# A squared-ReLU MLP in split float32: the second product turned round, 512 weight columns moving, and its halves alternated with the first product

## Chip, cores and metric

The kernel runs on one core of a Trainium2 chip. The metric is device time in microseconds, the median over runs of the whole program; the profile is one execution taken by the hardware profiler. Engines are named as the profile names them: PE (TensorE matmul), PEld (its weight loads), DVE (VectorE), ACT (ScalarE), POOL (GpSimd), SP (SyncE, which issues the loads).

## What is computed

One residual layer over 512 tokens of width 2048, in float32. Attention, a gated unit and their merge come first and are untouched. The end of the layer is the part that matters here:

```python
x = x + merged @ w_out[l]
h2 = rms_norm(x, g_ff[l])
x = x + jnp.square(jax.nn.relu(h2 @ w_ff1[l])) @ w_ff2[l]   # w_ff1 2048 x 8192, w_ff2 8192 x 2048
```

## The kernel before

Every float32 operand is split into a high and a low piece (`split_to`: ACT casts the high piece, DVE subtracts it from the source to get the low one), and each product is three matmuls, high*high, high*low and low*high (`mm3`, lines 64 to 66). So each line of `mm3` appears in the trace once for each product tile.

The program is written as straight Python loops; a tile framework places semaphores, gives out buffers and fixes the order on each engine ahead of the run. Buffers of 128 x 512 float32 come from one pool, `slots` (81 of them). Weights arrive in `w_raw` (three buffers), and their split pieces and sums live in `w_piece` (six buffers of 4 KB a partition). PSUM has eight banks, five `acc` and three `aux`.

The MLP walks the 8192 hidden columns in eight chunks of 1024, each of four pairs of 128-column blocks. `hidden(f, p)` makes one pair: `by_column` holds pieces of `w_ff1` (128 x 128) stationary and moves the 512 tokens of `h2T`; 96 matmuls; DVE applies the ReLU and the row scale out of PSUM (line 584), ACT squares. `factors` forms four further combinations of the pair's quarters on POOL (lines 596 to 599) and splits seven operands into `ys`.

`strassen` then does the second product as a two-by-two block product with seven block products instead of eight. It runs once for each chunk and each 256 output columns (eight passes a chunk, 64 in all). A pass loads eight 128-row blocks of `w_ff2` in two transfers, POOL adds the four weight sums (line 156), ACT and DVE split each of the seven weight operands (lines 99 and 100), and PE runs 7 x 4 x 3 = 84 matmuls: weight piece stationary, 256 tokens of `ys` moving, so the result is transposed (output column on the partition). After each block product DVE adds the PSUM result into `x2T`, the residual held transposed (line 624), one or two additions of 128 x 256. In the last chunk PE turns every finished block back (line 633), ACT copies it out of PSUM, and SP stores it. `x2T` is made earlier by `turned`: four transposes for each of 16 column blocks, which `h2T` needs too, and one ACT copy (line 562).

The first hidden pair of the next chunk is computed ahead of the passes of this one (`early`), so a chunk on PE is four `hidden` in a row and then eight passes in a row.

Of the kernel before, what the change touches and what calls it, by code (L numbers as in the profile page):

```python
# [9 lines left out]
F32 = mybir.dt.float32  # L10
F32R = mybir.dt.float32r
AF = mybir.ActivationFunctionType
ALU = mybir.AluOpType
AX = mybir.AxisListType

P = 128
D = 2048
S = 512
NTB = S // P
KT = D // P  # L20
# [5 lines left out]
EPS = 1e-6  # L26
CK = 2
W = 512


@with_exitstack
def tile_hybrid_layer(ctx: ExitStack, tc: tile.TileContext, x, g_mix, w_in, g_q, g_k, ln_g, ln_b,
# [4 lines left out]
    nc = tc.nc  # L37

    const = ctx.enter_context(tc.tile_pool(name="const", bufs=1))
    wpool = ctx.enter_context(tc.tile_pool(name="wpool", bufs=3))  # L40
    small = ctx.enter_context(tc.tile_pool(name="small", bufs=8))
    slots = ctx.enter_context(tc.tile_pool(name="slots", bufs=81))
    ps_acc = ctx.enter_context(tc.tile_pool(name="ps_acc", bufs=5, space=bass.MemoryType.PSUM))
    ps_aux = ctx.enter_context(tc.tile_pool(name="ps_aux", bufs=3, space=bass.MemoryType.PSUM))

    def slot(name, dt=F32):
        return slots.tile([P, 512], dt, name=name, tag="slot")

    def acc(name):
        return ps_acc.tile([P, 512], F32, name=name, tag="acc")  # L50

    def aux(name):
        return ps_aux.tile([P, 512], F32, name=name, tag="aux")
# [8 lines left out]
    def mm3(o, lh, rh, start, stop, **kw):  # L62

        nc.tensor.matmul(o, lhsT=lh[0], rhs=rh[0], start=start, stop=False, **kw)  # L64
        nc.tensor.matmul(o, lhsT=lh[0], rhs=rh[1], start=False, stop=False, **kw)  # L65
        nc.tensor.matmul(o, lhsT=lh[1], rhs=rh[0], start=False, stop=stop, **kw)  # L66

    state = {"load": None}
# [19 lines left out]
        nc.vector.tensor_tensor(out=lo, in0=raw, in1=f32(hi), op=ALU.subtract)  # L88
        return hi, lo

    def split(src, name, scale=None):

        hi, lo = slot(name + "_hi", F32R), slot(name + "_lo", F32R)
        split_to(hi, lo, src, scale)
        return hi, lo

    def split_to(hi, lo, src, scale=None):
        if scale is None:
            nc.scalar.copy(out=hi, in_=src)  # L99
            nc.vector.tensor_tensor(out=lo, in0=src, in1=f32(hi), op=ALU.subtract)  # L100
        else:
            nc.scalar.activation(out=hi, in_=src, func=AF.Copy, scale=scale)
            nc.vector.scalar_tensor_tensor(out=lo, in0=src, scalar=scale, in1=f32(hi),
                                           op0=ALU.mult, op1=ALU.subtract)

    early = []
# [26 lines left out]
        for c in range(w // P):  # L133
            evac(c, o[c])

    def strassen(wap, r0, c0, rhs, evac):

        KH = 4
        half = []
        for h in range(2):
            raw = wpool.tile([P, KH, 2, P], F32, name="w_raw", tag="w_raw", bufs=3)
            state["load"] = nc.sync.dma_start(
                out=raw.rearrange("p k h c -> p k (h c)"),
                in_=wap[r0:r0 + 2 * KH * P, c0:c0 + 2 * P].rearrange("(k h p) c -> h p k c", p=P, h=2)[h])
            half.append(raw)  # L150
        w11, w21 = half[0][:, :, 0, :], half[0][:, :, 1, :]
        w12, w22 = half[1][:, :, 0, :], half[1][:, :, 1, :]
        sums = [wpool.tile([P, 2, KH, P], F32, name="w_sum", tag="w_piece", bufs=6) for _ in range(2)]
        sa, sc, sd, sb = sums[0][:, 0], sums[0][:, 1], sums[1][:, 0], sums[1][:, 1]
        for o, a, b in ((sa, w11, w21), (sc, sa, w22), (sd, sc, w12), (sb, w21, w22)):
            nc.gpsimd.tensor_tensor(out=o, in0=a, in1=b, op=ALU.add)  # L156
        banks = [acc("q") for _ in range(4)]
        for w, name, b, first, last in ((w11, "y11", 0, True, False), (w12, "y21", 1, True, True),
                                        (sa, "m7", 2, True, False), (sc, "m6", 0, False, False),
                                        (sd, "y22", 3, True, True), (w22, "m4", 2, False, True),  # L160
                                        (sb, "m5", 0, False, True)):
            both = wpool.tile([P, 2, KH, P], F32R, name="w_both", tag="w_piece", bufs=6)
            split_to(both[:, 0], both[:, 1], w)
            o = banks[b][:, :2 * P]
            for k in range(KH):
                mm3(o, (both[:, 0, k, :], both[:, 1, k, :]), rhs(k, name), first and k == 0, k == KH - 1,
                    skip_group_check=True)
            evac(name, o)


    warm = const.tile([P, 1], F32, name="warm")
# [2 lines left out]
    ident = const.tile([P, P], F32, name="ident")  # L174
# [76 lines left out]
    def hT_of(k):  # L251

        if k == len(hT):
            t = aux("xT")
            for tb in range(NTB):
                nc.tensor.transpose(out=t[:, tb * P:(tb + 1) * P], in_=xq[tb, k], identity=ident)
            hT.append(split(t, "hT", gT[:, k:k + 1]))
        return hT[k]

    def scale_of_x():  # L260
# [262 lines left out]
    for j in range(D // W):  # L523
        g = gb.pop(0) if gb else gate(GA + D + j * W, "gb")
        flush()

        def evac_b(c, o):
            m = slot("merged")
            nc.vector.tensor_tensor(out=m, in0=o, in1=g[c], op=ALU.mult)
            nc.gpsimd.tensor_tensor(out=m, in0=m, in1=merged_a[j * 4 + c], op=ALU.add)  # L530
            mT.append(split(m, "mT"))

        by_column(w_ob[0], j * W, lambda k: sT[k], SGW // P, evac_b, "yb")


    x2 = {}
    x2T = []
    h2T = []
    ss2 = const.tile([P, NTB, 4], F32, name="ss2")
    for j in range(D // W):  # L540
        def evac_x(tb, o):
            t = x2[tb, j]
            nc.vector.tensor_tensor(out=t, in0=o, in1=t, op=ALU.add)
            sq = slot("sq")
            nc.scalar.activation(out=sq, in_=t, func=AF.Square, accum_out=ss2[:, tb, j:j + 1])

        ref = state["load"]
        with tc.issue_after(ref.ins):
            for tb in range(NTB):
                t = slot("x2")  # L550
                nc.sync.dma_start(out=t, in_=x[tb * P:(tb + 1) * P, j * W:(j + 1) * W])
                x2[tb, j] = t
        by_token(w_out[0], j * W, lambda k: mT[k], KT, evac_x, "xo")

        def turned(c, j=j):
            t = aux("x2T")
            for tb in range(NTB):
                nc.tensor.transpose(out=t[:, tb * P:(tb + 1) * P], in_=x2[tb, j][:, c * P:(c + 1) * P],
                                    identity=ident)
            k = j * 4 + c  # L560
            keep = slot("x2T")
            nc.scalar.copy(out=keep, in_=t)
            x2T.append(keep)
            h2T.append(split(t, "h2T", gT2[:, k:k + 1]))

        behind.extend([lambda c=c, turned=turned: turned(c) for c in range(4)])
# [3 lines left out]
    rstd2 = rsqrt(ms2, 4, "rstd2")  # L570
    behind.append(lambda: along(rstd2, rstd_b))


    HS = S // 2
    PAIRS = 4
    chunks = DFF // (PAIRS * 2 * P)

    def hidden(f, p):
# [26 lines left out]
            split_to(*y[name], src)  # L605
        return y

    early = hidden(0, 0)
    for f in range(chunks):
        ys = [factors(early)]  # L610
        ys += [factors(hidden(f, p)) for p in range(1, PAIRS)]
        if f < chunks - 1:

            early = hidden(f + 1, 0)
        for j in range(D // (2 * P)):
            ca, cb = x2T[2 * j], x2T[2 * j + 1]
            a11, a12, a21, a22 = ca[:, :HS], ca[:, HS:], cb[:, :HS], cb[:, HS:]
            takes = {"y11": [(a11, ALU.add)], "y21": [(a11, ALU.add)], "m7": [(a22, ALU.add)],
                     "m6": [(a21, ALU.subtract)], "y22": [(a12, ALU.add)], "m4": [(a21, ALU.add)],
                     "m5": [(a22, ALU.subtract), (a12, ALU.add)]}  # L620

            def evac_y(name, o):
                for a, op in takes[name]:
                    nc.vector.tensor_tensor(out=a, in0=a, in1=o, op=op)  # L624

            strassen(w_ff2[0], f * PAIRS * 2 * P, j * 2 * P, lambda k, name: ys[k][name], evac_y)
            if f == chunks - 1:
                for pb in range(2):
                    t = aux("xo")
                    for b in range(2):  # L630
                        for c in range(2):
                            tb = pb * 2 + b
                            nc.tensor.transpose(out=t[:, (b * 2 + c) * P:(b * 2 + c + 1) * P],
                                                in_=(ca, cb)[c][:, tb * P:(tb + 1) * P], identity=ident)
                    r = slot("out")
                    nc.scalar.copy(out=r, in_=t)
                    nc.sync.dma_start(
                        out=out[pb * 2 * P:(pb + 1) * 2 * P, j * 2 * P:(j + 1) * 2 * P]
                        .rearrange("(b p) c -> p b c", p=P),
                        in_=r.rearrange("p (b c) -> p b c", b=2))  # L640


# [23 lines left out]
```

## Time and profile before

| what | us |
|---|---|
| median of three runs (2591.97 to 2593.3) | 2592.62 |
| the profiled execution | 2592.95 |
| its span, first to last instruction | 2591.2 |

The span is what the rows below are measured in; the profiled execution's own time is 1.75 us more than its span. Engine "busy" is the union of instruction times. Matmuls overlap in the records (a new one starts before the record of the last one ends), so the pace of PE is read from start to start and not from the mean duration.

### The profile page before, as it was taken

The numbers are of one execution on the slowest core, as the hardware profiler recorded it, in microseconds if no ns is written. First come the engines' busy times: TensorE is split into PE (matmuls) and PEld (weight loads), VectorE is DVE, ScalarE is ACT, GpSimd is POOL, SyncE is SP. The second block draws the span as 40 slices with busy tenths as digits, with TensorE's granted clock in tenths as the row PEclk, the third lists the DMA queues.
The fourth block names the chain that finished last, engine by engine and source line by source line (L and its number), as shares of the span: only waits on it lengthen the run. The fifth ranks groups of instructions, "written<-read, shape, count | busy, mean of one in ns | idle before, by whom it ended". The sixth has DMA issues, their size and how long they took to land.

```text
span 2591.2 us, 34954 instructions
## 1 busy us (share of the span) xinstructions
PE 2572.0 (99%) x14058; PEld 2235.7 (86%) x14058; DVE 1399.7 (54%) x2030; ACT 906.7 (35%) x1428; POOL 606.6 (23%) x507
## 2 busy tenths in 40 slices
PE   8999999999999999999999999999999999999999
PEld 7888888888888888888899898898998988989989
DVE  4555563333335333333567486584774856847666
ACT  5333342222223222233333343343333433433334
POOL 0211110000201100000143252351522624415233
PEclk9999999999999999999999999999999999999999
DMA  5332322333332333433333333233232332333333
GB/s 171 90 90 74 90 72 91 97 98 98 114 112 84 98 98 98 129 107 107 97 86 115 93 90 114 84 104 110 87 114 90 99 113 83 115 98 90 112 90 117
DMA packets 204419, 260.24 MB, mean 100 GB/s; under 512 B 8368, under 2 KB 146656, under 8 KB 204256
## 3 DMA queue, kind: packets, MB, share of 16 engines
q1 hardware_dynamic: 204256, 258.01, 33.3%
q8 instruction: 110, 1.80, 0.3%
q14 instruction: 53, 0.43, 0.1%
HBM read 253.78 MB, written 4.19 MB: 100 GB/s over the span
## 4 chain that ended last, share of the span: by engine, by line
PE 97%; DVE 2%; issue 0%; DMA 0%; ACT 0%; SPq 0%; POOL 0%; DVEq 0%; ACTq 0%; POOLq 0%
PE q L64 9%; PE q L66 9%; PE q L65 9%; PE f L65 9%; PE f L66 9%; PE f L64 9%; PE xo L66 2%; PE xo L64 2%; PE xo L65 2%; PE gb L64 2%; PE gb L65 2%; PE gb L66 2%; PE ga L64 2%; PE ga L66 2%; PE ga L65 2%; PE v L66 1%
## 5 line engine op out<-in xcount | busy, mean ns | idle before, releaser
L88 DVE TENSOR_TENSOR w_lo<-w_raw,w_hi 128x1024 fp32r<-128x1024 f32 x336 | 415.4, 1236 | 826.5 <-ACT w_hi L86 813.1
L86 ACT CAST w_hi<-w_raw 128x1024 fp32r<-128x1024 f32 x336 | 353.6, 1052 | 951.5 <-PE f L65 248.4
L64 PE MATMUL q<-ys,w_both 128*128 128x256 f32 x1792 | 505.4, 285 | 3.0 <-DVE x2T L624 0.6
L65 PE MATMUL q<-ys,w_both 128*128 128x256 f32 x1792 | 501.8, 283 | 0.1
L66 PE MATMUL q<-ys,w_both 128*128 128x256 f32 x1792 | 491.1, 284 | 3.5 <-DVE w_both L100 3.5
L64 PE MATMUL f<-h2T_hi,w_hi 128*128 128x512 f32 x1024 | 398.7, 389 | 0.0
L65 PE MATMUL f<-h2T_lo,w_hi 128*128 128x512 f32 x1024 | 398.4, 389 | 0.0
L66 PE MATMUL f<-h2T_hi,w_lo 128*128 128x512 f32 x1024 | 397.4, 389 | 0.0
L64 PEld LDWEIGHTS q<-ys,w_both 128*128 128x128 f32 x1792 | 342.9, 191 | 10.4 <-issue 8.9
L65 PEld LDWEIGHTS q<-ys,w_both 128*128 128x128 f32 x1792 | 343.3, 192 | 0.8 <-DVE ys L100 0.3
L66 PEld LDWEIGHTS q<-ys,w_both 128*128 128x128 f32 x1792 | 335.4, 192 | 6.8 <-DVE w_both L100 6.8
L156 POOL TENSOR_TENSOR w_sum<-w_raw 128x512 f32<-128x512 f32 x128 | 185.0, 1452 | 261.3 <-PE q L66 169.1
L624 DVE TENSOR_TENSOR x2T<-x2T,q 128x256 f32<-128x256 f32 x512 | 198.6, 410 | 78.5 <-PE q L66 77.4
L100 DVE TENSOR_TENSOR w_both<-w_raw,w_both 128x512 fp32r<-128x512 f32 x192 | 193.3, 1030 | 67.5 <-ACT w_both L99 67.5
L65 PEld LDWEIGHTS f<-h2T_lo,w_hi 128*128 128x128 f32 x1024 | 192.2, 188 | 39.7
L66 PEld LDWEIGHTS f<-h2T_hi,w_lo 128*128 128x128 f32 x1024 | 192.2, 188 | 39.6
L64 PEld LDWEIGHTS f<-h2T_hi,w_hi 128*128 128x128 f32 x1024 | 192.3, 188 | 39.4
L100 DVE TENSOR_TENSOR w_both<-w_sum,w_both 128x512 fp32r<-128x512 f32 x256 | 217.5, 869 | 1.3 <-ACT w_both L99 1.2
L99 ACT CAST w_both<-w_sum 128x512 fp32r<-128x512 f32 x256 | 157.8, 619 | 171.5 <-PE q L66 133.5
L99 ACT CAST w_both<-w_raw 128x512 fp32r<-128x512 f32 x192 | 118.1, 621 | 227.4 <-PE q L66 113.4
L156 POOL TENSOR_TENSOR w_sum<-w_sum,w_raw 128x512 f32<-128x512 f32 x128 | 183.1, 1431 | 5.0
L596 POOL TENSOR_TENSOR m<-relu 128x256 f32<-128x256 f32 x32 | 37.0, 1158 | 596.7 <-ACT relu L585 596.7
(202 smaller groups left out, 4088.3 us busy)
## 6 DMA issues: line engine op xcount, KB each, us to landing
w_raw<-in_w_ff_dram SPq DMA_DIRECT2D x256, 512.0 KB, 4.0
w_raw<-in_w_in_dram SPq DMA_DIRECT2D x144, 512.0 KB, 3.8
w_raw<-in_w_out_dram SPq DMA_DIRECT2D x32, 512.0 KB, 3.8
w_raw<-in_w_oa_dram SPq DMA_DIRECT2D x16, 512.0 KB, 3.8
w_raw<-in_w_ob_dram SPq DMA_DIRECT2D x16, 512.0 KB, 3.7
x<-in_x_dram SPq DMA_DIRECT2D x16, 256.0 KB, 5.0
out_dram<-out SPq DMA_DIRECT2D x16, 256.0 KB, 4.5
xq<-in_x_dram SPq DMA_DIRECT2D x12, 256.0 KB, 5.5
```

What stands on the lines that cost most here:

```text
L64: nc.tensor.matmul(o, lhsT=lh[0], rhs=rh[0], start=start, stop=False, **kw)
L65: nc.tensor.matmul(o, lhsT=lh[0], rhs=rh[1], start=False, stop=False, **kw)
L66: nc.tensor.matmul(o, lhsT=lh[1], rhs=rh[0], start=False, stop=stop, **kw)
L86: nc.scalar.copy(out=hi, in_=raw)
L88: nc.vector.tensor_tensor(out=lo, in0=raw, in1=f32(hi), op=ALU.subtract)
L99: nc.scalar.copy(out=hi, in_=src)
L100: nc.vector.tensor_tensor(out=lo, in0=src, in1=f32(hi), op=ALU.subtract)
L156: nc.gpsimd.tensor_tensor(out=o, in0=a, in1=b, op=ALU.add)
L596: nc.gpsimd.tensor_tensor(out=m7, in0=y12, in1=y22, op=ALU.subtract)
L624: nc.vector.tensor_tensor(out=a, in0=a, in1=o, op=op)
```

## The change

The second product now holds the activations stationary, 128 tokens at a time, and moves 512 columns of weights, so that a result lies token on the partition, as `x2` itself lies. A chunk is two pairs (512 hidden columns, 16 chunks); the block product is now over two halves of the tokens and two 512-column halves of a 1024-column output half, so there are two passes a chunk (`g` = 0, 1), 32 in all. A pass is 7 block products x 2 token tiles x 2 pairs x 3 = 84 matmuls of 512 columns. It loads four quarters of `w_ff2` (128 x 2 x 512 each) into a new pool `whole` of five buffers; the four weight sums are made on POOL one by one, three of them in place over a quarter, each before the operand that needs it. Each block product has two PSUM results of 128 x 512, each added by DVE into `x2` in one or two additions (16 in a pass). `x2T` with its copies, the final transposes and the copies out are gone; the stores go from `x2`. The order is `hidden` of the next chunk's first pair, pass 0 of this chunk, `hidden` of the second pair, pass 1. `slots` shrinks to 72; ten buffers of a pool `spare` hold the first pieces of `hT` and the last of `mT`, and their room is given to `whole` afterwards.

```diff
+SLOTS = 72
+SPARE = 10
...
-    def strassen(wap, r0, c0, rhs, evac):
-        KH = 4
-        half = []
-        for h in range(2):
-            raw = wpool.tile([P, KH, 2, P], F32, name="w_raw", tag="w_raw", bufs=3)
...
-        for o, a, b in ((sa, w11, w21), (sc, sa, w22), (sd, sc, w12), (sb, w21, w22)):
-            nc.gpsimd.tensor_tensor(out=o, in0=a, in1=b, op=ALU.add)
-        banks = [acc("q") for _ in range(4)]
...
-            both = wpool.tile([P, 2, KH, P], F32R, name="w_both", tag="w_piece", bufs=6)
-            split_to(both[:, 0], both[:, 1], w)
-            o = banks[b][:, :2 * P]
-            for k in range(KH):
-                mm3(o, (both[:, 0, k, :], both[:, 1, k, :]), rhs(k, name), first and k == 0, k == KH - 1,
-                    skip_group_check=True)
-            evac(name, o)
+    def strassen(wap, r0, c0, lhs, evac):
+        KH = 2
+        def piece(name):
+            return wpool.tile([P, KH, W], F32R, name=name, tag="w_piece", bufs=6)
+        def whole(name):
+            return state["whole"].tile([P, KH, W], F32, name=name, tag="whole")
+        def quarter(h, c):
+            raw = whole("w_raw")
             state["load"] = nc.sync.dma_start(
+                out=raw, in_=wap[r0:r0 + 2 * KH * P, c0 + c * W:c0 + (c + 1) * W]
+                .rearrange("(k h p) c -> h p k c", p=P, h=2)[h])
+            return raw
+        w11, w12, w21, w22 = quarter(0, 0), quarter(1, 0), quarter(0, 1), quarter(1, 1)
+        sc = whole("w_sum")
+        def plus(o, a, b):
             nc.gpsimd.tensor_tensor(out=o, in0=a, in1=b, op=ALU.add)
+        made = {"m7": lambda: plus(w11, w11, w21), "m6": lambda: plus(sc, w11, w22),
+                "y22": lambda: plus(w12, sc, w12), "m5": lambda: plus(w21, w21, w22)}
+        take = {"y11": w11, "y21": w12, "m7": w11, "m6": sc, "y22": w12, "m4": w22, "m5": w21}
+        banks = {}
+        for name, b, first, last in (("y11", 0, True, False), ("y21", 1, True, True),
+                                     ("m7", 2, True, False), ("m6", 0, False, False),
+                                     ("y22", 1, True, True), ("m4", 2, False, True),
+                                     ("m5", 0, False, True)):
+            if name in made:
+                made[name]()
+            hi, lo = piece("w_hi"), piece("w_lo")
+            split_to(hi, lo, take[name])
+            if first:
+                banks[b] = [(aux if b == 1 else acc)("q") for _ in range(2)]
+            for t in range(2):
+                o = banks[b][t]
+                for k in range(KH):
+                    y = [part[:, t * P:(t + 1) * P] for part in lhs(k, name)]
+                    mm3(o, y, (hi[:, k, :], lo[:, k, :]), first and k == 0, k == KH - 1,
+                        skip_group_check=True)
+                evac(name, t, o)
...
-            keep = slot("x2T")
-            nc.scalar.copy(out=keep, in_=t)
-            x2T.append(keep)
...
+    before.close()
+    state["whole"] = ctx.enter_context(tc.tile_pool(name="whole", bufs=5))
...
-    PAIRS = 4
+    PAIRS = 2
...
+    takes = {"y11": [(0, 0, ALU.add)], "y21": [(0, 0, ALU.add)], "m7": [(1, 1, ALU.add)],
+             "m6": [(0, 1, ALU.subtract)], "y22": [(1, 0, ALU.add)], "m4": [(0, 1, ALU.add)],
+             "m5": [(1, 1, ALU.subtract), (1, 0, ALU.add)]}
+    ahead = [hidden(0, p) for p in range(PAIRS)]
     for f in range(chunks):
...
+        ys = [factors(act) for act in ahead]
+        ahead = []
+        for g in range(2):
+            if f < chunks - 1:
+                ahead.append(hidden(f + 1, g))
+            def evac_y(name, t, o):
+                for half, c, op in takes[name]:
+                    a = x2[2 * half + t, 2 * g + c]
                     nc.vector.tensor_tensor(out=a, in0=a, in1=o, op=op)
...
-            if f == chunks - 1:
-                for pb in range(2):
-                    t = aux("xo")
...
+                    if f == chunks - 1 and (name, half, c) in (("m4", 0, 1), ("y21", 0, 0),
+                                                              ("m5", 1, 1), ("m5", 1, 0)):
+                        tb, j = 2 * half + t, 2 * g + c
+                        nc.sync.dma_start(out=out[tb * P:(tb + 1) * P, j * W:(j + 1) * W], in_=a)
+            strassen(w_ff2[0], f * PAIRS * 2 * P, g * 2 * W, lambda k, name: ys[k][name], evac_y)
```

## Rows read from the trace of the kernel before

**Rows 1.** The page's busy times by engine (share of the span, number of instructions) and its line of the granted TensorE clock in 40 slices, 9 being full speed.

```profile
PE 2572.0 (99%) x14058; PEld 2235.7 (86%) x14058; DVE 1399.7 (54%) x2030; ACT 906.7 (35%) x1428; POOL 606.6 (23%) x507
...
PEclk9999999999999999999999999999999999999999
```

**Rows 2.** The page's chain of work that ended last, shares of the span by engine; and what PE waited for in the whole span: total us, times, longest us.

```profile
PE 97%; DVE 2%; issue 0%; DMA 0%; ACT 0%; SPq 0%; POOL 0%; DVEq 0%; ACTq 0%; POOLq 0%
...
PE q L66 <- DVE w_both L100: 3.5, 9, 2.0
```

**Rows 3.** The matmuls of the first product (f) and of the second (q), by tile: number, duration ns min/median/max, first and last start, shape.

```profile
L64 PE MATMUL f<-h2T_hi,w_hi x1024: 389/389/473, 1215.2 to 2493.4; 128*128 128x512 f32 x171
...
L66 PE MATMUL f<-h2T_hi,w_lo x1024: 389/389/478, 1215.7 to 2493.8; 128*128 128x512 f32 x171
...
L66 PE MATMUL q<-ys,w_both x1792: 277/283/387, 1327.0 to 2585.5; 128*128 128x256 f32 x200
```

**Rows 4.** PE in order of time (start us, duration us): the first and the last of 92 successive matmuls of 512 columns, of which the earlier ones (xo) hold activations and move weights and the later ones (f) hold weights and move activations.

```profile
1199.82 0.39 PE L65 MATMUL xo<-w_lo,mT_hi 128*128 128x512 f32 x1
...
1220.44 0.40 PE L66 MATMUL f<-h2T_hi,w_lo 128*128 128x512 f32 x1
```

**Rows 5.** PE in order of time: the first and the last of 19 successive matmuls of 256 columns in a pass.

```profile
1504.74 0.28 PE L66 MATMUL q<-ys,w_both 128*128 128x256 f32 x1
...
1506.90 0.28 PE L64 MATMUL q<-ys,w_both 128*128 128x256 f32 x1
```

**Rows 6.** The chain of work that ended last, in order of time (start us, us): starts of passes of the first chunk (two of them four passes apart), then the last chunk with its final transposes, and the end.

```profile
1355.04 0.36 PE q L64
...
1396.50 0.35 PE q L64
...
2523.55 0.44 PE xo L633 x4
...
2578.25 0.44 PE xo L633 x4
2585.78 0.42 DVE x2T L624
...
2587.35 0.59 ACT out L636
```

**Rows 7.** Groups of instructions by line and shape: count, busy us, mean ns of one, idle time before them and what ended it.

```profile
L88 DVE TENSOR_TENSOR w_lo<-w_raw,w_hi 128x1024 fp32r<-128x1024 f32 x336 | 415.4, 1236 | 826.5 <-ACT w_hi L86 813.1
L86 ACT CAST w_hi<-w_raw 128x1024 fp32r<-128x1024 f32 x336 | 353.6, 1052 | 951.5 <-PE f L65 248.4
...
L156 POOL TENSOR_TENSOR w_sum<-w_raw 128x512 f32<-128x512 f32 x128 | 185.0, 1452 | 261.3 <-PE q L66 169.1
L624 DVE TENSOR_TENSOR x2T<-x2T,q 128x256 f32<-128x256 f32 x512 | 198.6, 410 | 78.5 <-PE q L66 77.4
L100 DVE TENSOR_TENSOR w_both<-w_raw,w_both 128x512 fp32r<-128x512 f32 x192 | 193.3, 1030 | 67.5 <-ACT w_both L99 67.5
...
L100 DVE TENSOR_TENSOR w_both<-w_sum,w_both 128x512 fp32r<-128x512 f32 x256 | 217.5, 869 | 1.3 <-ACT w_both L99 1.2
...
L156 POOL TENSOR_TENSOR w_sum<-w_sum,w_raw 128x512 f32<-128x512 f32 x128 | 183.1, 1431 | 5.0
...
L100 DVE TENSOR_TENSOR ys<-m,ys 128x256 fp32r<-128x256 f32 x128 | 71.1, 579 | 4.6 <-ACT ys L99 4.6
L100 DVE TENSOR_TENSOR ys<-relu,ys 128x256 fp32r<-128x256 f32 x96 | 70.0, 749 | 1.4 <-ACT ys L99 1.4
...
L584 DVE SCALAR_TENSOR_TENSOR relu<-f,rstd_b 128x512 f32<-128x512 f32 x64 | 44.3, 692 | 87.0 <-PE f L66 86.9
...
L543 DVE TENSOR_TENSOR x<-xo,x 128x512 f32<-128x512 f32 x16 | 11.0, 690 | 5.5 <-PE xo L66 4.0 <-DMA w_raw<-in_w_out_dram 0.7 <-DMA w_raw<-in_w_ff_dram 0.7
```

**Rows 8.** Three stretches: length, and for each engine its busy time and instructions, then granted clock, DMA share, GB/s. The first is four `hidden` with a pass at its end, the second passes alone, the third the last chunk's passes.

```profile
1413.00:1506.00 93.00, 93.00 (x449) 78.62 (x448) 43.44 (x58) 31.73 (x54) 24.01 (x23) 1.00 0.31 95
1506.00:1582.00 76.00, 75.48 (x607) 73.72 (x607) 68.78 (x115) 32.73 (x55) 37.61 (x26) 1.00 0.35 105
2494.00:2591.00 97.00, 89.59 (x738) 87.85 (x736) 67.48 (x126) 43.46 (x78) 40.08 (x32) 1.00 0.36 109
```

**Rows 9.** DVE and POOL in order of time within one pass: a split with no POOL instruction beside it, POOL's sums, and two splits that ran beside them.

```profile
1542.68 0.68 DVE L100 TENSOR_TENSOR w_both<-w_raw,w_both 128x512 fp32r<-128x512 f32 x1
...
1546.43 3.01 POOL L156 TENSOR_TENSOR w_sum<-w_sum,w_raw 128x512 f32<-128x512 f32 x2
...
1547.57 2.41 DVE L100 TENSOR_TENSOR w_both<-w_raw,w_both 128x512 fp32r<-128x512 f32 x2
```

**Rows 10.** DVE in order of time through one `hidden`: weight splits as pieces come free, and the ReLU of the same half of two successive `hidden`.

```profile
1421.49 1.23 DVE L88 TENSOR_TENSOR w_lo<-w_raw,w_hi 128x1024 fp32r<-128x1024 f32 x1 [4.21 <-ACT w_hi L86]
1426.93 1.23 DVE L88 TENSOR_TENSOR w_lo<-w_raw,w_hi 128x1024 fp32r<-128x1024 f32 x1 [4.21 <-ACT w_hi L86]
1428.79 0.69 DVE L584 SCALAR_TENSOR_TENSOR relu<-f,rstd_b 128x512 f32<-128x512 f32 x1 [0.64 <-PE f L66]
...
1450.55 0.69 DVE L584 SCALAR_TENSOR_TENSOR relu<-f,rstd_b 128x512 f32<-128x512 f32 x1 [0.63 <-PE f L66]
```

**Rows 11.** DMA issues: size and median us from issue to landing.

```profile
w_raw<-in_w_ff_dram SPq DMA_DIRECT2D x256, 512.0 KB, 4.0
...
out_dram<-out SPq DMA_DIRECT2D x16, 256.0 KB, 4.5
```

More of the change, by code (lines that the diff above doesn't have):

```diff
@@ L41, in tile_hybrid_layer, with slot @@
     small = ctx.enter_context(tc.tile_pool(name="small", bufs=8))
-    slots = ctx.enter_context(tc.tile_pool(name="slots", bufs=81))
+    slots = ctx.enter_context(tc.tile_pool(name="slots", bufs=SLOTS))
+    before = ExitStack()
+    spare = before.enter_context(tc.tile_pool(name="spare", bufs=SPARE))
     ps_acc = ctx.enter_context(tc.tile_pool(name="ps_acc", bufs=5, space=bass.MemoryType.PSUM))
     ps_aux = ctx.enter_context(tc.tile_pool(name="ps_aux", bufs=3, space=bass.MemoryType.PSUM))
-    def slot(name, dt=F32):
-        return slots.tile([P, 512], dt, name=name, tag="slot")
+    def slot(name, dt=F32, pool=slots):
+        return pool.tile([P, 512], dt, name=name, tag="slot")
     def acc(name):
@@ L89, in weight, with split @@
         return hi, lo
-    def split(src, name, scale=None):
-        hi, lo = slot(name + "_hi", F32R), slot(name + "_lo", F32R)
+    def split(src, name, scale=None, pool=slots):
+        hi, lo = slot(name + "_hi", F32R, pool), slot(name + "_lo", F32R, pool)
         split_to(hi, lo, src, scale)
@@ L134, in by_column @@
             evac(c, o[c])
-    def strassen(wap, r0, c0, rhs, evac):
-        KH = 4
-        half = []
-        for h in range(2):
-            raw = wpool.tile([P, KH, 2, P], F32, name="w_raw", tag="w_raw", bufs=3)
-            state["load"] = nc.sync.dma_start(
[L148 to L154, printed above, removed]
-        for o, a, b in ((sa, w11, w21), (sc, sa, w22), (sd, sc, w12), (sb, w21, w22)):
-            nc.gpsimd.tensor_tensor(out=o, in0=a, in1=b, op=ALU.add)
-        banks = [acc("q") for _ in range(4)]
[L158 to L161, printed above, removed]
-            both = wpool.tile([P, 2, KH, P], F32R, name="w_both", tag="w_piece", bufs=6)
-            split_to(both[:, 0], both[:, 1], w)
-            o = banks[b][:, :2 * P]
-            for k in range(KH):
-                mm3(o, (both[:, 0, k, :], both[:, 1, k, :]), rhs(k, name), first and k == 0, k == KH - 1,
-                    skip_group_check=True)
-            evac(name, o)
@@ L256, in hT_of @@
                 nc.tensor.transpose(out=t[:, tb * P:(tb + 1) * P], in_=xq[tb, k], identity=ident)
-            hT.append(split(t, "hT", gT[:, k:k + 1]))
+            hT.append(split(t, "hT", gT[:, k:k + 1], spare if k < SPARE // 2 else slots))
         return hT[k]
@@ L530, in evac_b @@
             nc.gpsimd.tensor_tensor(out=m, in0=m, in1=merged_a[j * 4 + c], op=ALU.add)
-            mT.append(split(m, "mT"))
+            mT.append(split(m, "mT", pool=spare if len(mT) >= KT - 4 else slots))
         by_column(w_ob[0], j * W, lambda k: sT[k], SGW // P, evac_b, "yb")
     x2 = {}
-    x2T = []
     h2T = []
@@ L606, in factors @@
         return y
-    early = hidden(0, 0)
+    takes = {"y11": [(0, 0, ALU.add)], "y21": [(0, 0, ALU.add)], "m7": [(1, 1, ALU.add)],
+             "m6": [(0, 1, ALU.subtract)], "y22": [(1, 0, ALU.add)], "m4": [(0, 1, ALU.add)],
+             "m5": [(1, 1, ALU.subtract), (1, 0, ALU.add)]}
+    ahead = [hidden(0, p) for p in range(PAIRS)]
     for f in range(chunks):
[L610 to L623, printed above, removed]
-                    nc.vector.tensor_tensor(out=a, in0=a, in1=o, op=op)
-            strassen(w_ff2[0], f * PAIRS * 2 * P, j * 2 * P, lambda k, name: ys[k][name], evac_y)
-            if f == chunks - 1:
-                for pb in range(2):
-                    t = aux("xo")
[L630 to L640, printed above, removed]
```

## Prediction, made before the changed kernel was run

> **What bounds the kernel now.** I read the shares of the engines first, then the chain that ended last and PE's waits, then the pace of PE from start to start, and last what the other engines do in the stretches of the second product. PE is busy 99% of the span at the full granted clock [rows 1], the chain is PE for 97%, and its largest wait in this product is 3.5 us in nine pieces, for DVE's weight splits [rows 2]. So time is gained only by giving PE less to do, and lost only where another engine makes PE wait.
>
> The pace is the point. 92 matmuls of 512 columns start within 20.62 us: 20.62 / 91 = 0.2266 us each, and this series runs over both orientations (weights moving, then activations moving) without a break [rows 4]. 19 matmuls of 256 columns take 2.16 us: 2.16 / 18 = 0.1200 us each [rows 5]. Two of these cost 0.2400 us, one wide one 0.2266 us: a matmul carries 13.4 ns that do not scale with its columns. A pass is 84 x 0.1200 = 10.08 us, but passes follow each other every (1396.50 - 1355.04) / 4 = 10.365 us [rows 6], so 0.285 us is lost at each pass. A `hidden` takes 1450.55 - 1428.79 = 21.76 us [rows 10], which is 96 x 0.2267.
>
> The other engines have slack on average and little inside the passes: DVE is busy 68.78 of 76 us there, and 43.44 of 93 us in the stretch of `hidden` [rows 8].
>
> **PE's share, worked out.** The multiplications are the same: 64 passes x 84 matmuls x 256 columns against 32 x 84 x 512. Before: 64 x 10.365 = 663.4 us. After: a pass is 84 x 0.2266 = 19.03 us, and I leave it the same loss at its start, 0.285 us, since it has as many instructions: 32 x 19.32 = 618.2 us. That is -45.2 us. The bounds are no loss per pass (-54.3) and 0.39 us more at each of some 31 changes from `hidden` to a pass, which is what the nine waits of 3.5 us make each [rows 2] (-45.2 + 12 = -33).
>
> The eight blocks of the last chunk are 10.94 us apart, (2578.25 - 2523.55) / 5, instead of 10.365 [rows 6]: the final transposes cost 8 x 0.575 = 4.6 us, and they go: -4.6 us. The 16 ACT copies into `x2T` and the ACT copies of the output go too; ACT is not on the chain [rows 2], so they are worth nothing. The 64 transposes into h2T stay, as does all of the first product.
>
> The weights of the MLP are the same bytes, in transfers of the same 512 KB that land in 4.0 us [rows 11]; at a third of the DMA engines [rows 8] they stay hidden. SP's queue now has a pass's four quarters between the loads of two `hidden`: they wait for `whole` buffers, which the last pass gives back between its third product and its end, a whole `hidden` (21.76 us) ahead of their need. Earlier stages keep as many `slots` as before: 81 less 32 of hT against 72 less 22, and the last eight pieces of mT lie in `spare`. I cost this at nothing, with 2 us to either side.
>
> **DVE, the engine that could spoil it.** Splits: seven of 128 x 1024 a pass in place of fourteen of 128 x 512. One of that size takes 1.236 us with POOL still [rows 7], and up to 2 x 1.2 = 2.4 us beside POOL's sums, since two of 512 columns took 2.41 us there, against 0.68 us for one alone [rows 9]; the means of 1.030 and 0.869 us over 448 splits make 0.917, or 1.83 us for the double size [rows 7]. Additions: 16 of 128 x 512 a pass, 0.690 us each by the same form at line 543, 11.0 us, where two old passes had 16 of 0.410 us, 6.6 us [rows 7]. So DVE gets 4.4 us more a pass, 143 us in all. One `hidden` and one pass on PE take 21.76 + 19.32 = 41.1 us; DVE's work in that time is 7 x 1.83 + 11.0 for the pass, 4 x 1.236 + 2 x 0.692 for the `hidden`, and 4 x 0.579 + 3 x 0.749 for one pair's `ys` [rows 7]: 12.8 + 11.0 + 6.3 + 4.6 = 34.7 us, 85%. On average it fits.
>
> Inside a pass I laid the work out in order. Six `w_piece` buffers are three pairs, and a block product takes PE 12 x 0.2266 = 2.72 us, so a pair comes free every 2.72 us and its successor is needed 5.44 us after that. At the pass's start two pairs stand ready: the preceding `hidden` uses a pair for 5.44 us [rows 10], which leaves them time. From there DVE does one split (1.24) and two additions (1.38) for each 2.72 us, the four additions of the last product falling into the next `hidden`. The third operand's split would end at about 3.3 us beside POOL's last sum, need 5.44; the fourth at 5.9, need 8.16; the fifth at 8.6, need 10.9; the sixth at 11.2, need 13.6; the seventh at 13.8, need 16.3. All have about 2.4 us in hand. The other sums fall into the `hidden` ahead, once the first operands are split. The splits and additions just fit into the pass; the `ys` must wait for the next `hidden`, which has the room. Even if the third operand's split had to wait out a whole sum of 2.9 us, it would be ready at 4.3 us. Hence no lasting stall in a period, but a thin margin.
>
> At the end there is no `hidden` to take the overflow: three passes stand in a row, the last of chunk 14 and the two of chunk 15. DVE's work: 21 splits at 1.236 (26.0), 48 additions (33.1), one pair's `ys` (4.6), and 0.6 us more for each of the 14 splits of two passes that run beside POOL (8.4), less two splits done early (2.5): 69.6 us against 3 x 19.32 = 58.0 on PE. I take 12 us of stall; the bounds are 0 and, with the other pair's `ys` late too, 16. The kernel before has a stall there as well: from the last f at 2493.8 to the last q at 2585.5 [rows 3] are 91.7 us, eight blocks less the last transposes 86.9: 4.8 us. Net +7.2 us. After the last matmul: before, 2591.2 - 2585.6 = 5.6 us; after, two additions (1.4) and a store (about 4.5 [rows 11]), 5.9: nothing.
>
> One rule of the Trainium skill speaks against the wider sums. The row: two sums and two splits that overlapped took 3.01 and 2.41 us, where one split alone takes 0.68 [rows 9]. "SBUF — State Buffer" (section "SBUF: two separate sides") calls the port pair that VectorE and GpSimd share an exclusive lock, held for a whole instruction; the row agrees. A sum now lasts some 2.9 us, twice 1.44, so by that rule a split that meets one waits half of it on average, 1.45 us an estimate: eight sums in the last two passes would cost 11.6 us where I count 8.4 above, and the time would be 2550 us by the rule against 2547 by the rows.
>
> **Sum.** -45.2 - 4.6 + 7.2 - 3.5 (the old waits for splits) = -46.1 us on the profiled execution's 2592.95, its span plus 1.75: 2546.9. The median is 0.3 us less, so **2547 us**. Its own range: with neither losses at passes nor at the end, 2592.6 - 54.3 - 4.6 - 4.8 - 3.5 = 2525; with the upper bounds, 2592.6 - 33 - 4.6 + 11.2 = 2566.
>
> **Rivals.**
> *Thin margins leak.* The `ys` splits and factor sums get in among the pass's own on DVE's and POOL's queues: 4.6 us more in a pass against 2.4 us in hand costs up to 2.2 us in the passes that meet it, say half of them: 16 x 2.2 = 35 us, 2582. For it: additions already queue behind splits in the old passes (90% busy [rows 8]). Against: those passes lost only 0.285 us.
> *No gain per column.* If a wide matmul of this product took twice a narrow one, 0.2400 us, the 2688 x 0.0134 = 36 us that the wide step saves would be gone: 2583. "TensorE: Matmul & The Clock Gate" (section "Back-to-back issue gap") gives about 2.5 ns as the fixed part of a matmul, and by it the step alone would save only some 7 us, and the sum would be 2576, an estimate from the page; rows 4 and 5 show 13.4 ns and decide against it, in either orientation.
> *Slower: DVE becomes the bound.* Only three pairs of pieces are ahead, so DVE's work may not move out of the pass. In it DVE needs 7 x 1.83 + 11.0 + 0.7 = 24.5 us against PE's 19.32: 5.2 us a pass, of which half may still fall into the `hidden`: 32 x 2.6 = 83 us, 2630; all of it, 2713. It decides from 46 / 32 = 1.4 us a pass. For it: DVE's 90% in passes now, and 68% more time for additions. Against: `hidden` after each pass leaves DVE half idle [rows 8], and PE waits 3.5 us in all today.
>
> **Chances.** Forecast 0.67, leak 0.18, no gain per column 0.03, DVE bound 0.12. What a measurement here can tell is about 0.2%, 5 us. Faster by more: 0.86; within: 0.03; slower: 0.11. Range 2525 to 2583: it takes in the forecast, the leak and the third case, and leaves the DVE bound out.
>
> **What would show it.** q matmuls of 512 columns 0.2266 us apart, passes of 19.0 to 19.5 us, PE's waits for splits (line of the low piece) under 15 us before the last three passes, and some 12 us within them; DVE near 95% in passes and near 70% in `hidden`; additions at 0.69 us and splits between 1.24 and 2.4 us. Wrong if PE waits for `w_lo` over 1.4 us in each pass, if the wide q matmuls stand 0.24 us apart, or if the stages up to 1215 us move by more than 2 us.

## The result, and the profile after

The changed kernel takes 2573.95 us (median; 2573.24 to 2574.19) against 2592.96 us for the kernel before on the same chip: a ratio of 0.9926, 95% interval 0.9909 to 0.9943. It is faster by 19 us; 46 were forecast. The time lies inside the range given, near the rival called "thin margins leak".

The page of the changed kernel: its busy times, its chain of work that ended last, and the groups that matter. What was line 64 to 66 is 68 to 70 here, the splits of a pass are line 104, the additions line 643, POOL's weight sums line 165.

```profile
span 2572.5 us, 28610 instructions
PE 2532.1 (98%) x11306; PEld 2082.1 (81%) x11306; DVE 1438.7 (56%) x1806; ACT 852.9 (33%) x1172; POOL 589.0 (23%) x379
...
PE 87%; DVE 10%; issue 1%; ACT 1%; DMA 0%; POOL 0%; SPq 0%; DVEq 0%; ACTq 0%; POOLq 0%
...
L104 DVE TENSOR_TENSOR w_lo<-w_raw,w_hi 128x1024 fp32r<-128x1024 f32 x192 | 281.9, 1469 | 255.8 <-ACT w_hi L103 255.8
...
L643 DVE TENSOR_TENSOR x<-x,q 128x512 f32<-128x512 f32 x512 | 331.0, 676 | 2.3 <-PE q L70 0.6
```

PE's share of the chain fell from 97% [rows 2] to 87%, DVE's rose from 2% to 10%: PE now waits, and for DVE. Its waits in the span (total us, times, longest us) say for what, with 26.3 us where rows 2 had 3.5:

```profile
PE q L69 <- DVE w_lo L104: 26.3, 34, 1.8
```

Six of the 34 lie behind the last f; the others make two in each of 14 chunks.

Where in a chunk this happens is to be seen in the chain in order of time (start us, us). The same steps return after 1828.54 - 1744.51 = 84.03 us:

```profile
1744.51 1.06 ACT w_hi L103
1745.60 1.84 DVE w_lo L104
1747.55 1.11 DVE x L643 x2
1748.74 1.26 DVE w_lo L104
1750.01 0.88 DVE ys L104
1751.42 3.04 DVE ys L104 x4
1755.73 1.14 DVE w_lo L104
1758.40 0.67 DVE ys L104 x2
1759.59 1.22 DVE w_lo L104
1828.54 1.06 ACT w_hi L103
```

PE needs 2 x 21.76 + 2 x 19.04 = 81.6 us for a chunk, so 2.43 us are lost, and the chain leaves PE for some 16 us in one of the two passes only, the second. The first pass has no gap: there every product stands 2.72 us behind the last. A first pass, a second pass and the `hidden` behind it, in the form of rows 8 (length, then busy time and instructions of PE, PEld, DVE, ACT and POOL), show how DVE is loaded:

```profile
1703.90:1722.70 18.80, 18.80 (x84) 15.58 (x83) 17.77 (x21) 7.72 (x9) 1.84 (x1) 1.00 0.44 139
1744.50:1766.20 21.70, 20.18 (x87) 15.79 (x85) 21.29 (x32) 12.32 (x23) 10.41 (x9) 1.00 0.32 97
1766.20:1787.70 21.50, 21.50 (x95) 17.75 (x95) 10.83 (x13) 4.83 (x5) 8.42 (x4) 1.00 0.32 98
```

In the second pass DVE is busy 21.29 of 21.70 us, in the `hidden` behind it 10.83 of 21.50: the room is there, and the work is not in it. DVE in order of time in a second pass shows what is different:

```profile
1748.74 1.26 DVE L104 TENSOR_TENSOR w_lo<-w_sum,w_hi 128x1024 fp32r<-128x1024 f32 x1
1749.93 0.95 DVE L104 TENSOR_TENSOR ys<-relu,ys 128x256 fp32r<-128x256 f32 x1
1750.81 0.67 DVE L643 TENSOR_TENSOR x<-x,q 128x512 f32<-128x512 f32 x1
1751.41 0.41 DVE L104 TENSOR_TENSOR ys<-relu,ys 128x256 fp32r<-128x256 f32 x1
1751.74 1.84 DVE L104 TENSOR_TENSOR ys<-m,ys 128x256 fp32r<-128x256 f32 x2
1753.51 0.96 DVE L104 TENSOR_TENSOR ys<-relu,ys 128x256 fp32r<-128x256 f32 x1
1754.39 0.68 DVE L643 TENSOR_TENSOR x<-x,q 128x512 f32<-128x512 f32 x1
1754.98 0.75 DVE L104 TENSOR_TENSOR ys<-m,ys 128x256 fp32r<-128x256 f32 x2
1755.66 1.21 DVE L104 TENSOR_TENSOR w_lo<-w_raw,w_hi 128x1024 fp32r<-128x1024 f32 x1
```

Between two weight splits of the pass stand seven operand splits (`ys`) of the next chunk, 4.9 us of them, several at 0.95 us where one alone takes 0.41. ACT had cast the fifth operand's high piece at 1752.15 to 1753.20; DVE comes to the low piece at 1755.66. PE waits for it: this is the late split. ACT was itself held for 1.43 us before that, by one of POOL's combinations whose cast stands ahead on its queue (ACT, then PE):

```profile
1750.64 0.41 ACT L103 CAST ys<-m 128x256 fp32r<-128x256 f32 x1 [1.43 <-POOL m L616]
...
1752.15 1.05 ACT L103 CAST w_hi<-w_raw 128x1024 fp32r<-128x1024 f32 x1
...
1756.92 0.50 PE L69 MATMUL q<-w_lo,ys 128*128 128x512 f32 x1 [0.94 <-DVE w_lo L104]
```

POOL at the same time runs all eight combinations of `factors`, for both pairs, since the code calls `factors` for both behind the second pass (three of them):

```profile
1748.89 1.72 POOL L616 TENSOR_TENSOR m<-m,relu 128x256 f32<-128x256 f32 x1
1750.68 0.81 POOL L617 TENSOR_TENSOR m<-relu,m 128x256 f32<-128x256 f32 x1
1751.44 0.98 POOL L615 TENSOR_TENSOR m<-relu 128x256 f32<-128x256 f32 x1
```

So theory A: the factor work of the next chunk falls as a whole into the second pass and makes that pass's own splits late. Its rivals were that a pass is overfull by itself (B), that factor work costs its full time wherever it stands (C), that ACT's queue is what is late (D), and within A, whether DVE's time (A1) or POOL's hold on it (A2) does the harm.

### The profile page after: what moved, and what is told of

Its sections match the earlier page's. It is cut to its first block, busy times and chain, and to the rows that moved or that the text cites. A ratio compares the mean times of both kernels' runs of the same rounds, so it can differ in the third digit from the quotient of the medians.

```text
span 2572.5 us, 28610 instructions
## 1 busy us (share of the span) xinstructions
PE 2532.1 (98%) x11306; PEld 2082.1 (81%) x11306; DVE 1438.7 (56%) x1806; ACT 852.9 (33%) x1172; POOL 589.0 (23%) x379
## 4 chain that ended last, share of the span: by engine, by line
PE 87%; DVE 10%; issue 1%; ACT 1%; DMA 0%; POOL 0%; SPq 0%; DVEq 0%; ACTq 0%; POOLq 0%
PE f L69 9%; PE f L68 9%; PE f L70 9%; PE q L69 6%; PE q L70 6%; PE q L68 6%; DVE w_lo L104 4%; DVE ys L104 3%; DVE x L643 3%; PE xo L70 2%; PE xo L69 2%; PE xo L68 2%; PE gb L68 2%; PE gb L70 2%; PE gb L69 2%; PE ga L68 2%
## 5 line engine op out<-in xcount | busy, mean ns | idle before, releaser
L92 DVE TENSOR_TENSOR w_lo<-w_raw,w_hi 128x1024 fp32r<-128x1024 f32 x336 | 414.2, 1233 | 686.5 <-ACT w_hi L90 677.7
L90 ACT CAST w_hi<-w_raw 128x1024 fp32r<-128x1024 f32 x336 | 353.7, 1053 | 988.8 <-PE q L69 190.0
L104 DVE TENSOR_TENSOR w_lo<-w_raw,w_hi 128x1024 fp32r<-128x1024 f32 x192 | 281.9, 1469 | 255.8 <-ACT w_hi L103 255.8
L69 PE MATMUL q<-w_lo,ys 128*128 128x512 f32 x896 | 352.8, 394 | 26.4 <-DVE w_lo L104 26.3
L165 POOL TENSOR_TENSOR w_raw<-w_raw 128x1024 f32<-128x1024 f32 x64 | 183.1, 2862 | 820.0 <-DVE w_lo L104 820.0
L70 PE MATMUL q<-w_hi,ys 128*128 128x512 f32 x896 | 349.0, 389 | 0.0
L643 DVE TENSOR_TENSOR x<-x,q 128x512 f32<-128x512 f32 x512 | 331.0, 676 | 2.3 <-PE q L70 0.6
L103 ACT CAST w_hi<-w_raw 128x1024 fp32r<-128x1024 f32 x192 | 201.8, 1053 | 391.2 <-PE f L69 290.3
L68 PE MATMUL q<-w_hi,ys 128*128 128x512 f32 x896 | 324.0, 391 | 1.5 <-DVE x L643 1.2
L69 PEld LDWEIGHTS q<-w_lo,ys 128*128 128x128 f32 x896 | 168.1, 188 | 74.1 <-DVE w_lo L104 40.0
L68 PEld LDWEIGHTS q<-w_hi,ys 128*128 128x128 f32 x896 | 168.1, 188 | 40.3 <-issue 3.5
L70 PEld LDWEIGHTS q<-w_hi,ys 128*128 128x128 f32 x896 | 168.3, 188 | 33.8
L68 PE MATMUL xo<-w_hi,mT_hi 128*128 128x512 f32 x256 | 100.5, 393 | 0.0
L68 PE MATMUL ga<-hT_hi,w_hi 128*128 128x512 f32 x256 | 100.4, 392 | 0.0
```

Source lines behind the costliest of these rows:

```text
L90: nc.scalar.copy(out=hi, in_=raw)
```

## The experiments

**Without the factor work.**

```diff
-        ys = [factors(act) for act in ahead]
+        if f == 0:
+            ys = [factors(act) for act in ahead]
```

> Starts from the changed kernel and leaves out the work of `factors` (8 POOL combinations, 14 splits) for every chunk but the first, whose operands are used again, so the second product is not computed. Theory A (the factor work, which falls as a whole into the second pass of each chunk, pushes that pass's own weight splits past their need; 84.03 us from chunk to chunk where PE needs 2 x 21.76 + 2 x 19.03 = 81.6): the chunks come at 81.6 to 81.9 us, 15 x 2.2 = 33 us and some 3 us of the end are gained, about 2538 us, no wait of PE for w_lo in a second pass. Rival B (splits and 16 additions alone already fill DVE in a pass): at least half the waits stay, 2555 us or more.

Measured: 2534.36 us, ratio 0.9771 (0.9756 to 0.9785). PE's waits for the low pieces shrank to

```profile
PE q L69 <- DVE w_lo L104: 2.6, 3, 1.9
```

all of them at the end. From the first f (1215.0) to the last (2465.6) are 1250.6 us; 32 `hidden` of 21.76 and 29 passes of 19.04 make 1248.5, and the transposes into h2T and a few other small matmuls that stand among the first f take the rest. No pass loses anything, and B falls: splits and additions alone fit.

**Combinations without splits.** `factors` returns behind its POOL instructions in every chunk but the first.

```diff
...
+        if not whole_job:
+            return None
...
+        else:
+            for act in ahead:
+                factors(act, False)
```

> As the run without `factors`, but the 8 POOL combinations of every chunk are made and only the 14 splits are left out (the operands of the first chunk are used again, so the second product is not computed). Within theory A it separates DVE's and ACT's time from POOL's hold on DVE. A1 (the splits' own time, 14 x 0.4 to 0.9 us on DVE, is the load): within 4 us of the run without `factors`, about 2540 us. A2 (POOL's combinations, 8 x 0.8 to 1.7 us in the pass, block DVE's splits beside them): most of the loss stays, 2560 us or more.

Measured: 2533.95 us (ratio 0.9770, 0.9755 to 0.9784), no more than without either. POOL's combinations by themselves cost nothing, though they run in the same place and slowly (the second pair's first one takes 1.73 us where 0.98 was seen above). A2 in its plain form is out.

**The work spread over both passes.**

```diff
-        ys = [factors(act) for act in ahead]
+        ys = made_ahead if f else [factors(act) for act in ahead]
+        made_ahead = []
...
             strassen(w_ff2[0], f * PAIRS * 2 * P, g * 2 * W, lambda k, name: ys[k][name], evac_y)
+            if f < chunks - 1:
+                made_ahead.append(factors(ahead[g]))
```

> The changed kernel with `factors` of the next chunk's first pair called behind the first pass and of the second pair behind the second pass, instead of both behind the second pass; nothing else. Theory A: a pass then meets 7 splits and 4 combinations instead of 14 and 8; about 4 us of DVE work against 2.4 us in hand and the next `hidden` behind it, so most of the 2.4 us a chunk goes: 2545 to 2555 us. Rival C (any factor work among a pass's own on the queues costs its full time): the loss is only divided over both passes, 1.2 us each, 2570 to 2575 us.

Measured: 2535.98 us, ratio 0.9778 (0.9762 to 0.9795): 38 us faster than the changed kernel, 58 faster than the kernel before, with the whole computation done. It did better than expected (2545 to 2555): nothing is left of the loss between the first f and the last, and C is out. Its chain returns to the same f every 40.80 us, which is 21.76 + 19.04:

```profile
2326.99 0.45 PE f L70 x2
2367.79 0.45 PE f L70 x2
2408.59 0.45 PE f L70 x2
```

In its passes the seven operand splits lie one or two at a time between the pass's own instructions:

```profile
1736.37 0.67 DVE L644 TENSOR_TENSOR x<-x,q 128x512 f32<-128x512 f32 x1
1736.97 1.29 DVE L104 TENSOR_TENSOR ys<-relu,ys 128x256 fp32r<-128x256 f32 x2
1738.19 0.67 DVE L644 TENSOR_TENSOR x<-x,q 128x512 f32<-128x512 f32 x1
1738.79 1.21 DVE L104 TENSOR_TENSOR w_lo<-w_raw,w_hi 128x1024 fp32r<-128x1024 f32 x1
1739.92 0.74 DVE L104 TENSOR_TENSOR ys<-m,ys 128x256 fp32r<-128x256 f32 x2
```

**All of DVE's part moved behind the pass.**

```diff
+        if 0 < f < chunks - 1:
+            with tc.issue_after(state["added"].ins):
+                ys = [factors(act) for act in ahead]
+        else:
+            ys = [factors(act) for act in ahead]
...
+                    state["added"] = nc.vector.tensor_tensor(out=a, in0=a, in1=o, op=op)
```

> The changed kernel with both `factors` of chunks 1 to 14 queued on DVE behind the last addition of the second pass, so that DVE's 14 splits fall into the `hidden` that follows; POOL's combinations and ACT's casts stay free to come early. Theory A1 (DVE's time in the pass): the waits of the second pass go, 2540 to 2548 us. Rival D (ACT's casts of the operands stand before the weight casts on ACT's queue, and that is what is late): the waits stay, 2570 us.

Measured: 2540.89 us, ratio 0.9796 (0.9781 to 0.9810). The 14 splits run in one row in the `hidden` (second and third line below), and no pass before the last f loses; the 5 us over the spread version lie behind the last f, 66.7 us where that has 62.7, and behind the last q. ACT still casts `ys` ahead of the weights, which makes DVE wait 2.03 us for a cast (first line) without PE noticing: ACT's lateness alone costs nothing, and D falls.

```profile
1740.07 1.62 DVE L104 TENSOR_TENSOR w_lo<-w_raw,w_hi 128x1024 fp32r<-128x1024 f32 x1 [2.03 <-ACT w_hi L103]
...
1753.32 0.74 DVE L104 TENSOR_TENSOR ys<-relu,ys 128x256 fp32r<-128x256 f32 x2
...
1757.35 0.75 DVE L104 TENSOR_TENSOR ys<-m,ys 128x256 fp32r<-128x256 f32 x2
```

**Fourteen splits in every pass.** In the spread version:

```diff
             split_to(*y[name], src)
+            split_to(*y[name], src)
```

> The version with `factors` spread over both passes, with every split of an operand done twice (ACT's cast and DVE's subtraction; the same values again): 14 splits in each pass, as the changed kernel has in its second pass, but with 4 POOL combinations instead of 8. Theory A1 (DVE's splits in a pass against some 2.4 us in hand): each pass loses what the second pass lost, up to 2.4 us, 30 x 1.2 to 2.4 = 36 to 72 us, 2572 to 2608 us. Rival F (it was the order, both pairs called together, and not the amount): no more than 5 us over the spread version, 2541 us.

Measured: 2549.27 us, ratio 0.9829 (0.9813 to 0.9846), between the two expectations: 13 us over the spread version. From the first f to the last, 2475.2 - 1214.1 = 1261.1 us, it is 10.6 over it: 0.37 us on average for each of 29 passes, not 2.4, and 2.6 of the 10.6 fall into the first pass alone (the ReLU of successive `hidden` at 1282.32 and 1325.75, 43.43 us apart in place of 40.80). Fourteen splits beside four combinations thus explain about a sixth of the loss, and A1 in its plain form is out, too.

**Fourteen splits without POOL's combinations.** In the changed kernel, behind the first chunk:

```diff
...
+        else:
+            m7, m6, m4, m5 = y12, y22, y21, y11
...
```

> The changed kernel with all 14 operand splits of every chunk behind the second pass, as it has them, but without POOL's 8 combinations after the first chunk: four of the seven splits of a pair take a plain quarter instead, so the second product is wrong. The runs so far: the combinations alone cost nothing (2534 us), 14 splits with 4 combinations in each pass cost 0.43 us a pass, both together 2.43 us. J (the two act together: the splits beside a combination last 0.95 instead of 0.41 us and the combinations hold the first splits back): most of the loss goes, 2540 to 2548 us. K (14 splits called together are enough, by their place on the queue): the loss stays, 2565 us or more.

Measured: 2546.24 us, ratio 0.9819 (0.9805 to 0.9834). From the first f to the last, 2473.7 - 1214.1 = 1259.6 us, 9.0 over the version without the factor work: 0.64 us for each of 14 second passes, where the changed kernel loses (2500.1 - 1215.4 - 1250.6) / 14 = 2.44. So it takes both together: the eight combinations alone cost nothing, the 14 splits alone 0.64, and splits beside combinations 2.44 us. That is what J says, but this run changes two things at once. No operand split of the pass shown lasts 0.95 us, and the order is another, too: seven of the splits, which have no combination to wait for, come before the pass's fourth weight split (at 1741.44) and two between it and the fifth, where the changed kernel has seven:

```profile
1738.23 1.42 DVE L104 TENSOR_TENSOR ys<-relu,ys 128x256 fp32r<-128x256 f32 x4
...
1741.44 1.21 DVE L104 TENSOR_TENSOR w_lo<-w_sum,w_hi 128x1024 fp32r<-128x1024 f32 x1
```

**The alternation undone.**

```diff
+        if f < chunks - 1:
+            ahead = [hidden(f + 1, p) for p in range(PAIRS)]
         for g in range(2):
-            if f < chunks - 1:
-                ahead.append(hidden(f + 1, g))
```

> The changed kernel without the alternation: both `hidden` of the next chunk and then both passes of this one; all else as it is. If the alternation is what keeps DVE's work under PE (41 us on PE for 35 on DVE): two passes in a row need 14 x 1.24 + 32 x 0.68 + 14 operand splits of 0.4 to 0.9, 47 us or more on DVE against 38.1 on PE, of which some 8 us fall beside the `hidden`: 3 to 5 us a chunk, 2580 to 2615 us. If the alternation is worth nothing: 2574 us, and less if the factor work, free to spread over both passes, does better than in one.

Measured: 2645.01 us, ratio 1.0197 (1.0182 to 1.0212), slower than the kernel before and 30 us beyond the range expected. Chunks come 89.2 and 88.3 us apart by turns (the same split starts at 1929.03, 2018.26 and 2106.58), 7.2 over PE's need on average. PE's waits, and a stretch of two passes in the form of rows 8:

```profile
PE q L69 <- DVE w_lo L104: 32.7, 28, 1.9
PE q L68 <- ACT w_hi L103: 29.2, 29, 1.7
...
2017.30:2062.20 44.90, 41.23 (x171) 32.52 (x170) 44.63 (x57) 20.12 (x30) 22.33 (x13) 0.96 0.32 97
```

DVE is busy 44.63 of 44.90 us there: with two passes in a row, and the next chunk's splits among them, the wide second product makes DVE the bound. The alternation with `hidden` is worth 71 us and turns a loss into a gain.

**Where an old pass lost its 0.285 us.** Two attempts on the kernel before. The first took a fourth bank out of the `acc` pool's load:

```diff
-        banks = [acc("q") for _ in range(4)]
+        banks = [(aux if b == 1 else acc)("q") for b in range(4)]
```

> The kernel before with one edit: the PSUM result of the second block product (y21) of a pass comes from the `aux` banks instead of `acc`, so a pass takes three of the five `acc` banks instead of four. It tests what the 0.285 us at each old pass were. E1 (PE waits at a pass's start for a bank that the last additions of the pass before still hold): passes come every 84 x 0.1200 = 10.08 us and 64 x 0.285 = 18 us go, about 2574 to 2576 us. E2 (a cost of starting a pass, such as issuing): passes stay at 10.365 us, 2592 us.

Measured: 2593.53 us, ratio 0.9997 (0.9987 to 1.0006): nothing, so not that. The trace of before, DVE and then PE in order of time, shows PE start late in the middle of a pass, 0.35 us after the start of the matmul before it where 0.12 is the step, just behind the first of three additions, which itself stands behind a split that took 1.77 us beside POOL:

```profile
1543.29 1.77 DVE L100 TENSOR_TENSOR w_both<-w_sum,w_both 128x512 fp32r<-128x512 f32 x1
1544.98 1.07 DVE L624 TENSOR_TENSOR x2T<-x2T,q 128x256 f32<-128x256 f32 x3
...
1545.19 0.28 PE L66 MATMUL q<-ys,w_both 128*128 128x256 f32 x1
1545.54 0.35 PE L64 MATMUL q<-ys,w_both 128*128 128x256 f32 x1
```

The second left out the addition that the sixth product waits for:

```diff
-                     "m7": [(a22, ALU.add)],
+                     "m7": [],
```

> The kernel before without the addition of its third block product (m7) into the residual, so that this part is missing from the result; it tests again where the 0.285 us of an old pass went. G (the sixth product, m4, accumulates in the bank of m7 and must wait until DVE has added m7, which stands behind two splits on DVE's queue; only two narrow products of 1.44 us lie between): the wait goes, passes come every 10.08 us, 64 x 0.285 = 18 us less, 2574 to 2577 us. H (a cost of a pass that no addition makes): passes stay at 10.365 us, within 3 us of the kernel before.

Measured: 2591.28 us, ratio 0.9989 (0.9979 to 0.9999), where G expected 18 us less. That wait went, but others of some 0.1 us came in other products, so H, which expected no more than 3 us, has the number right and no cause shown. What sets the loss of an old pass stays open; that the wide passes have none is shown above, why is not.

## Why the prediction was wrong

- **The width of a matmul: right.** The wide step is 0.2266 us; a pass without waits is 19.04 us. Of the 663.4 us of the old passes 609.3 remain: 54.1 us gained, in full, in the spread version. Of these 36 us are the step (2688 x 13.4 ns). By the Trainium skill ("TensorE: Matmul & The Clock Gate", section "Back-to-back issue gap"), which gives 2.5 ns as the fixed part of the gap of an isolated matmul, the step would have been worth about 7 us, an estimate; the trace does not agree: here it is 13.4 ns.
- **The loss at each pass: a term too large.** "I leave it the same loss at its start, 0.285 us": the wide passes lose nothing. 32 x 0.285 = 9 us too little gain. Nor was it a loss at the start of a pass: the places of rows 6, 0.35 or 0.36 us long in the chain, are late starts in the middle of a pass like the one at 1545.54.
- **"The `ys` must wait for the next `hidden`, which has the room": this step failed.** The order on DVE let them into the second pass as soon as they were ready, both pairs at once, beside POOL's combinations. The hand-laid schedule was right for a pass without them (the first pass, and all passes of the run without factor work, have no gap), and right that DVE's average leaves room, more than the 85% worked out: in the changed kernel DVE is busy 57.99 of 84.00 us from 1744, 69%. It took for granted that work with room elsewhere goes there. Cost: 1284.7 us from first f to last in place of 1250.6, 34 us. The rival "thin margins leak" named this work, the margin and half the passes, and priced it at 35 us; 0.18 was too small a chance for it, given that nothing in the code held the splits back. That its price is so near is in part luck: it reckoned with one pair's splits in a pass, and the spread version, which has just that in every pass, loses nothing; it took both pairs in one pass, and POOL's combinations beside them.
- **The end: a term somewhat too large.** From the last f at 2500.6 to the last q at 2567.2 are 66.6 us for 57.1 of PE's work: 9.5 us of stall, 12 forecast. It is DVE, as expected (busy 67.11 of the 73 us from 2500 on): the spread version, too, has 2465.1 to 2527.8, 62.7 us.
- **The old waits: counted twice.** 3.5 us were taken off separately, but they lie within the passes: a chunk of before, 1505.76 - 1335.98 = 169.8 us between the same waits in the chain, less four `hidden` of 21.76 is 82.7 us for eight passes, no more than 8 x 10.365.
- **Sizes on DVE.** The mean of the 448 old splits is 0.938 us by their two means (192 x 1.030 and 256 x 0.869), not 0.917; that would be 1.88 us for the double size in place of 1.83. Both are too large for the changed kernel, where 192 of the 224 wide splits took 1.469 us on average and an addition 0.676. Only the 85% and the price of the rival that DVE becomes the bound hang on the 1.83.
- **The rival that DVE becomes the bound** did not come true for the change as it stands; without the alternation it does, at 2645 us. That its 2630 lies near is luck, since it was priced for passes with a `hidden` between them.

Together: -54 (passes) - 5 (final transposes) + 34 (factor work) + 5 (end, 9.5 against 4.8) = -20 us; measured -19. The Trainium skill ("SBUF — State Buffer", section "SBUF: two separate sides") calls the port pair that VectorE and GpSimd share an exclusive lock, held for a whole instruction; the changed kernel's trace agrees, with operand splits of 0.41 us at 0.95 beside POOL's combinations. I weighed it for the weight sums at the end of the kernel, and not for the factor work, where these longer splits stand.

## What to carry to other kernels

Average room on an engine is not enough: list what becomes ready in each stretch, and ask what on its queue holds it back; if nothing does, price it where it becomes ready, not where it would fit. When an operand is prepared for a whole chunk at once, spread its preparation over the chunk: calling `factors` once behind each pass, with the same instructions, was worth 38 us, twice what the whole change brought. And a product that gives DVE more to add can need another stage between its passes: here, without the alternation, it was slower than the kernel before by 2%.

## What the chip showed that was not expected

Two kinds of work that cost next to nothing alone cost almost four times their sum together: eight POOL combinations 0, fourteen DVE splits 0.64, both 2.44 us a pass, though the order on DVE was another in the run with the splits alone. That single splits grow from 0.41 to 0.95 us is in the trace; so are ACT's wait of 1.43 us for a combination and the seven splits that stand together ahead of the late weight split on DVE's queue, where the run without combinations has two. Which of these makes how much of the 2.44 us no run shows apart.
